# The attention's output projection as a streamed Strassen step, its weight sums made in DRAM, and the FFN's token halves exchanged

## The chip, the cores and the metric

The kernel runs on one core of a Trainium2 chip. The metric is the device time of one execution in microseconds (us), as the median of several. The engines are PE (TensorE: matrix products, and transposes by an identity), DVE (VectorE), ACT (ScalarE) and POOL (GpSimd); SP (SyncE) starts most transfers and does no arithmetic. Each engine works through its own list of instructions in order, and waits at an instruction until what it needs is there.

## The reference

One decoder block in fp32 on `x` of 1024 tokens by 1024 features, with a memory of 256 tokens:

```python
h = h + hybrid_mixer(rmsnorm(h, norm_mix), ...)              # two branches, merged @ w_o
h = h + mem_cross_attention(rmsnorm(h, norm_xattn), rmsnorm(mem, norm_mem), w_xq, w_xkv, w_xo)
h = h + swiglu(rmsnorm(h, norm_ffn), w_ffn_in, w_ffn_out)
return rmsnorm(h, norm_final)

def mem_cross_attention(n, m, w_xq, w_xkv, w_xo):            # 4 heads of 256
    q = (n @ w_xq).reshape(Bsz, S, 4, 256)
    k, v = jnp.split(m @ w_xkv, 2, axis=-1)
    s = jnp.einsum('bshd,bmhd->bhsm', q, k) * 256 ** -0.5
    p = jax.nn.softmax(s, axis=-1)
    o = jnp.einsum('bhsm,bmhd->bshd', p, v).reshape(Bsz, S, 1024)
    return o @ w_xo

def swiglu(n, w_ffn_in, w_ffn_out):
    g, u = jnp.split(n @ w_ffn_in, 2, axis=-1)
    return (jax.nn.silu(g) * u) @ w_ffn_out
```

The change concerns `o @ w_xo`, the residual sum behind it and the way into the FFN.

## The kernel before, in words

**Precision and layout.** Activations lie transposed, features on the 128 partitions and tokens along the row; a "half" is 512 tokens (`HALF`). Each operand of a product is split into a high part, rounded by ACT to PE's fast fp32 type, and a low part that DVE gets by subtraction (`split`, lines 227 to 233); a product is then three passes, high x high, high x low and low x high.

**Strassen.** Most of the large products are a Strassen-Winograd step: 2 x 2 blocks, seven block products (B11, B21, T1, B22, T2, T3, T4) in place of eight. `Wide` and its child `Stored` (lines 1222 to 1366) stream one for a 1024 x 1024 weight matrix: a product has two parts of 24 matmuls (`steps`), each prepared by `prep`, three parts ahead of PE: two DVE sums at most to form the right operand from quadrants (`COMB`), and a split of 128x1024 for either operand. `Stored` reads the sums of weight blocks that the products T1, T2, T3 and B22 need from a DRAM tensor, `sums_d`, that `weight_sums` (line 482) has filled by eight transfers on POOL's queue, twelve in fact since the accumulating ones are cut in two, each behind the one whose result it adds to. Each of the 28 results of 128x512 goes through `evac`: added on DVE onto its output quadrant (`home`), which starts as the block of the residual stream where there is one (`base`); when an output tile is complete, `post` is called. `w_o` goes that way (`wo`, with the mixer's input as base), and the attention's queries too (`xq`).

**The attention** (lines 1601 to 1675) goes over four heads, two token halves each: `score` (PE product, DVE maximum, ACT exponential, DVE division `pe<-pe,sm`), `turn` (PE transposes of the probabilities; then ACT and DVE split them to `phl`), `value` (PE product with `kvhl`; then `into` splits the result, ACT and DVE, into `hl`). The loop is staggered: in step n the scores of one head half, the transposes of the one before and the values of the one before that.

**Its output projection** (lines 1721 to 1725) is a plain product, `dense`: 16 output tiles of 128x512, 24 matmuls each. `Left` brings the weights in column pairs and splits them (`wd`, 128x1024), `residual` adds each result on DVE onto a tile `ga` of `h1_d`, stores it to `h2_d`, has ACT scale a copy for the FFN (`put_xo`, tiles `o`), and adds its square to the sum of squares `ssum` (`Stats.take`). `Stats` sends an add to POOL or DVE, whichever by the planner's running tally is free sooner.

**The FFN** takes its right operand from `Operands` (line 239; tiles B11h, B11l and so on: 28 steps, each a split and for some products a DVE combination); `B.upto(n)` makes steps ahead while the projection is running. Its weights are loaded by `Unit` and split to `whi` and `wlo` (`raw` and `sa` are the weights and their sums). `ffn_side` finishes the norm's statistics after a few of the FFN's steps.

**What sets the order.** The program is written out in Python in the order of its loops; within it `ahead()` raises the rank of an operation (splits, sums and evacuations of the streamed step), and `pinned` fixes one at its place. So the order in which DVE meets preparation, softmax and evacuation is a product of the scheduler. In the trace the DRAM tensors are shortened, `h_d` for `h1_d` and `h2_d`.

## Time and profile before

| what | value |
|---|---|
| time, median of 3 runs | 1927.17 us (1926.22 to 1928.36) |
| the profiled execution's own time | 1924.97 us |
| its span, first to last instruction | 1923.3 us |
| mean granted PE clock | 0.999 |
| PE busy | 1893.0 us, 98% of the span |
| DVE busy | 1361.0 us, 71% |
| ACT busy | 882.0 us, 46% |
| POOL busy | 515.0 us, 27% |
| the `w_xo` projection's matmuls on PE | 1172 to 1270 us, the first 77 among the last value products |

The profile's first part gives busy time, share of the span and number of instructions of each engine; the table by stage gives the same for a stretch of the execution, from:to in us, then its length, each engine's busy time with the count, the granted clock, the DMA engines' busy share and GB/s. A row of the groups has line, engine, operation, output<-input by the program's names, shapes and count; after the bar the summed busy time in us and the mean of one in ns, and after the second bar the engine's idle time just before such an instruction and what ended it. A row of the timeline has start, length, engine and the number of instructions alike in a row. A row of the chain of waits has start, length, and what was waited for.

### The profile page before, as it was taken

The page shows a single profiled execution, that of the slowest core. Times are in us where ns is not written, and L with a number is a line of the kernel's source. Part 1 is how long each engine was busy: PE and PEld are TensorE (multiplying, and loading weights), DVE is VectorE, ACT ScalarE, POOL GpSimd, SP SyncE. Part 2 cuts the span into 40 slices and gives each one's busy share as a digit, 9 for nine tenths or more (in the row PEclk, how much of TensorE's full clock was granted, in tenths as well). Part 3 has the DMA queues.
Part 4 walks back from the last instruction along what each step waited for, and adds up shares of the span by engine and source line. Part 5 has one row for each costly group of instructions (what it writes and reads, how often), then busy time and mean ns, then how long its engine had stood idle before and what let it go on. Part 6 is the DMA issues. An engine that isn't in the chain of part 4 may idle for free.

```text
span 1923.3 us, 26086 instructions
## 1 busy us (share of the span) xinstructions
PE 1893.0 (98%) x9680; PEld 1595.1 (83%) x9680; DVE 1361.0 (71%) x1948; ACT 882.0 (46%) x1521; POOL 515.0 (27%) x410
## 2 busy tenths in 40 slices
PE   7999999999999999999999999999999999999998
PEld 7998787888888888788888888888888888888888
DVE  7866879877776755553479685686878877866566
ACT  7534564564553444652136654553333333344243
POOL 0012324345444221001112000016454535330002
PEclk9999999999999999999999999999999999999999
DMA  9433383455643653898774510425666556397463
GB/s 344 147 95 102 127 306 107 147 177 178 192 154 121 208 181 115 313 328 227 216 191 133 194 58 4 156 98 139 190 174 153 158 168 168 111 300 257 163 220 122
DMA packets 240243, 333.70 MB, mean 174 GB/s; under 512 B 16346, under 2 KB 147652, under 8 KB 240116
## 3 DMA queue, kind: packets, MB, share of 16 engines
q1 hardware_dynamic: 223988, 290.09, 44.8%
q0 software_dynamic: 14400, 35.65, 9.2%
q10 hardware_dynamic: 1728, 6.29, 0.8%
q8 instruction: 76, 1.25, 0.3%
q14 instruction: 51, 0.42, 0.1%
HBM read 242.53 MB, written 120.91 MB: 189 GB/s over the span
## 4 chain that ended last, share of the span: by engine, by line
PE 86%; DVE 7%; issue 2%; DMA 2%; ACT 1%; POOL 1%; SPq 0%; POOLq 0%; DVEq 0%; ACTq 0%
PE acc L51 69%; PE bank L51 15%; DVE cv L73 2%; DVE wlo L73 2%; PE bank L55 2%; DVE o L73 1%; DVE hs L73 1%; DMA hl<-ys_d 0%; DMA zr<-sz_d 0%; DMA down_d<-in_w_ffn_out_dram 0%; POOL ssum L73 0%; ACT cv L783 0%; DMA sz_d<-zr 0%; DVE gy L73 0%; DMA mt<-in_mem_dram 0%
## 5 line engine op out<-in xcount | busy, mean ns | idle before, releaser
L73 DVE TENSOR_TENSOR wlo<-raw,whi 128x512 fp32r<-128x512 f32 x272 | 242.4, 899 | 99.7 <-ACT whi L232 99.7
L232 ACT ACTIVATE whi<-raw 128x512 fp32r<-128x512 f32 x272 | 169.4, 629 | 251.9 <-PE acc L51 210.1
L51 PE MATMUL acc<-hl,wd 128*128 128x512 f32 x1152 | 263.8, 390 | 1.7 <-ACT wd L232 1.3
L51 PEld LDWEIGHTS acc<-hl,wd 128*128 128x128 f32 x1152 | 215.5, 188 | 48.3 <-ACT wd L232 2.5
L73 DVE TENSOR_TENSOR o<-acc,o 128x512 f32<-128x512 f32 x244 | 167.0, 685 | 88.5 <-PE acc L51 85.7
L51 PE MATMUL acc<-fs 128*128 128x512 f32 (+1 forms) x792 | 155.7, 355 | 0.1
L51 PEld LDWEIGHTS acc<-fs 128*128 128x128 f32 x792 | 130.7, 189 | 20.8 <-issue 0.5
L73 DVE TENSOR_TENSOR fs<-fr,fs 128x1024 fp32r<-128x1024 f32 (+1 forms) x78 | 93.1, 1225 | 37.0 <-ACT fs L232 36.6
L232 ACT ACTIVATE fs<-fr 128x1024 fp32r<-128x1024 f32 (+1 forms) x78 | 74.3, 984 | 92.8 <-PE acc L51 27.4
L73 POOL TENSOR_TENSOR sa<-raw 128x512 f32<-128x512 f32 x43 | 68.4, 1592 | 146.2 <-DMA raw<-in_w_in_dram 75.4
L232 ACT ACTIVATE whi<-sa 128x512 fp32r<-128x512 f32 x96 | 59.8, 626 | 96.0 <-PE acc L51 92.7
L73 POOL TENSOR_TENSOR raw<-raw,sa 128x512 f32<-128x512 f32 x35 | 46.0, 1313 | 172.9 <-DVE wlo L73 172.9
L51 PE MATMUL acc<-ws 128*128 128x512 f32 x384 | 88.5, 389 | 0.0
L51 PEld LDWEIGHTS acc<-ws 128*128 128x128 f32 x384 | 72.0, 188 | 15.0
L51 PE MATMUL acc<-T4h,whi 128*128 128x512 f32 x192 | 76.3, 397 | 2.9 <-DVE o L73 2.9
L51 PE MATMUL acc<-B22h,wlo 128*128 128x512 f32 x192 | 75.7, 394 | 1.5 <-DVE wlo L73 1.5
L73 DVE TENSOR_TENSOR wlo<-sa,whi 128x512 fp32r<-128x512 f32 x96 | 70.9, 739 | 8.4 <-ACT whi L232 7.5
L51 PE MATMUL acc<-T1h,whi 128*128 128x512 f32 x192 | 76.2, 397 | 0.0
L51 PE MATMUL acc<-T3h,whi 128*128 128x512 f32 x192 | 76.0, 396 | 0.0
L51 PE MATMUL acc<-T2h,whi 128*128 128x512 f32 x192 | 75.8, 395 | 0.0
L51 PE MATMUL acc<-B22h,whi 128*128 128x512 f32 x192 | 75.7, 394 | 0.0
L73 POOL TENSOR_TENSOR rstd<-rstd,mhalf 128x4 f32<-128x4 f32 (+1 forms) x7 | 8.7, 1252 | 248.1 <-DVE rstd L73 248.1
(420 smaller groups left out, 5007.6 us busy)
## 6 DMA issues: line engine op xcount, KB each, us to landing
raw<-in_w_in_dram SPq DMA_DIRECT2D x26, 1024.0 KB, 5.8
raw<-in_w_ffn_in_dram SPq DMA_DIRECT2D x22, 1024.0 KB, 8.0
act_d<-o SPq DMA_DIRECT2D x77, 256.0 KB, 4.6
fr<-act_d SPq DMA_DIRECT2D x35, 512.0 KB, 7.6
down_d<-in_w_ffn_out_dram POOLq DMA_DIRECT2D x18, 768.0 KB, 7.2
fr<-down_d SPq DMA_DIRECT2D x20, 512.0 KB, 5.3
ga<-h_d SPq DMA_DIRECT2D x32, 256.0 KB, 3.6
csb<-cs_d SPq DMA_DIRECT2D x15, 512.0 KB, 4.3
```

What stands on the lines that cost most here:

```text
L51: return s.e.matmul(o, x, y, **kw)
L55: return s.e.transpose(o, x, i)
L73: return f(*a, **kw)
L232: pin(ACT.activation(hi, src, AF.Copy))
```

## The change

The weight sums for `w_xo` are made in a new DRAM tensor `xos_d` by the same twelve POOL transfers, started from step 3 of the query projection. The output projection becomes a `Stored` step `xo` with `h1_d` as base: `value` no longer splits its result but has ACT copy it into quadrants (`xo.rows`); the first two weight blocks are loaded in steps 3 and 4 of the attention, the first two parts prepared in steps 7 and 8. The output quadrant (1,0) lies in the former `ga` tiles, loaded one by one (`Row`). `post_xo` does what `residual` and `put_xo` did. The FFN's operands exchange the token halves (`swap=1`), so that they follow the order in which the Strassen step finishes its output, and are made two steps at a time from step 8 on. The FFN's first weight loads come one step sooner, its statistics two steps later, and the squares get six buffers (`Stats(rp, "ga", 6)`).

```diff
--- before.py
+++ after.py
@@ -103,6 +103,7 @@
     h1_d = dram("h1_d", D, TOK)
     h2_d = dram("h2_d", D, TOK)
     xqs_d = dram("xqs_d", 2 * D, HALF)
+    xos_d = dram("xos_d", 2 * D, HALF)
     xbc_d = dram("xbc_d", 1536, TOK)
     sz_d = dram("sz_d", D, TOK)
     q_d = dram("q_d", 512, TOK)
@@ -1218,6 +1219,14 @@
     HOME = ("aux", "aux", "m", "m")
     JS = (0, 1)
 
+    class Row:
+
+        def __init__(s, get):
+            s.get = get
+
+        def __getitem__(s, k):
+            return s.get(k[1] if isinstance(k, tuple) else k)
+
     class Wide:
 
 
@@ -1267,6 +1276,9 @@
                     s.plus(name, 2)
 
         def home(s, *ij, fill=True):
+            if ij not in s.keep and s.side[ij] == "ga":
+                s.keep[ij] = Row([quad(s.base, ij[0] * HALF + u * P, 0, ij[1]) for u in range(4)].__getitem__)
+                s.full.add(ij)
             if ij not in s.keep:
                 s.keep[ij] = slot(s.side[ij], (P, 4, HALF), name="wk")
             if fill and s.base is not None and ij not in s.full:
@@ -1364,6 +1376,9 @@
 
         def fetch(s, m, kp):
             s.load(*s.SEQ[:m + 3])
+            if s.base is not None:
+                for ij in {0: ((0, 0), (1, 1)), 2: ((0, 1),), 8: ((1, 0),)}.get(2 * m + kp, ()):
+                    s.home(*ij)
 
     class Left:
 
@@ -1431,7 +1446,7 @@
             yield
 
     EVEN, ODD = ("op",) * 8, ("op",) * 6 + ("aux",) * 2
-    i_ys, i_yg, i_q, i_xo = (paired(x) for x in (EVEN, ODD, EVEN, EVEN))
+    i_ys, i_yg, i_q = (paired(x) for x in (EVEN, ODD, EVEN))
 
     def fetch(src, dst, gain=None):
 
@@ -1522,14 +1537,6 @@
                 x.prep(ops.index(n) + 1, pin)
             yield
 
-    def residual(store, stats, gain, put, scale=1.0):
-        def post(o, j, p, q):
-            DVE.scalar_tensor_tensor(q, p, scale, q, ALU.mult, ALU.add)
-            SP.dma_start(store[o * P:(o + 1) * P, half(j)], q)
-            put(o, j, q, col(gain, o))
-            stats.take(j, q)
-        return post
-
     xq = Stored(t["w_xq"], lambda o, h, p, last: into(i_q, o, h, p, neg=last),
                 {"B11": "m", "T1": "m", "B21": "m", "*": "aux"}, {(0, 0): "m", (1, 1): "m", (0, 1): "aux"})
     xq.sums_d = xqs_d
@@ -1588,14 +1595,25 @@
         split_kv(es, pinned)
         yield
 
-    left_xo = Left((t["w_xo"],))
-
-    def next_left():
-        left_xo.upto(2)
-        yield
-
-    run(xq.steps(), (xq_side(), 1.0), (kv_side(), 1.0), (waiting(next_left(), 12), 1.0))
-    u_xo_stats = Stats(rp)
+    xsums = weight_sums([(t["w_xo"].rearrange("(j k p) c -> j p k c", j=2, p=P), xos_d, 4, 0)])
+    run(xq.steps(), (xq_side(), 1.0), (kv_side(), 1.0), (waiting(xsums, 3), 1.0))
+    drain(xsums)
+    u_xo_stats = Stats(rp, "ga", 6)
+    o_xo = {}
+
+    def row_xo(o):
+        if o // 2 not in o_xo:
+            o_xo[o // 2] = slot(HOME[o // 2], name="o")
+        return o_xo[o // 2][:, o % 2]
+
+    def post_xo(o, h, q, last):
+        SP.dma_start(h2_d[o * P:(o + 1) * P, half(h)], q)
+        ACT.activation(row_xo(o)[:, half(h)], q, AF.Copy, scale=col("norm_ffn", o))
+        u_xo_stats.take(h, q)
+
+    xo = Stored(t["w_xo"], post_xo, {"T2": "aux", "B21": "aux", "*": "m"},
+                {(0, 0): "m", (1, 1): "aux", (0, 1): "aux", (1, 0): "ga"}, h1_d)
+    xo.sums_d = xos_d
 
     class Att:
 
@@ -1652,7 +1670,7 @@
                     for x, y in ((kvh, ph), (kvl, ph), (kvh, pl_)):
                         PE.matmul(p, x[:, 2 + b, i * P:(i + 1) * P], y[:, b], start=m == 0, stop=m == 5)
                         m += 1
-                into(i_xo, 2 * s.h + i, s.j, p)
+                ACT.activation(xo.rows(2 * s.h + i, s.j), p, AF.Copy)
 
     pe = {}
     at = [Att(h, j) for h in range(4) for j in (1, 0)]
@@ -1672,6 +1690,10 @@
             b.turn(1)
         if a:
             a.score(1)
+        if n in (3, 4):
+            xo.load(xo.SEQ[n - 3])
+        if n in (7, 8):
+            xo.prep(n - 6)
 
 
     rbc2 = u_xo_stats.sum
@@ -1715,23 +1737,17 @@
         if u < 2:
             gate.e = up.e = DVE
         gu.append([gate, up])
-    o_xo = [slot(x, name="o") for x in HOME]
-    b_xo = blocks(o_xo)
-
-    def put_xo(o, j, q, g):
-        ACT.activation(b_xo[o][:, half(j)], q, AF.Copy, scale=g)
-
-    B = Operands(b_xo, 4, order=("B11", "T1", "B21", "B22", "T2", "T3", "T4"))
-    for n, _ in enumerate(dense(0, i_xo, residual(h2_d, u_xo_stats, "norm_ffn", put_xo), quad_of(h1_d), js=(1, 0), left=left_xo)):
+    B = Operands(lambda: Row(row_xo), 4, swap=1, order=("B11", "T1", "B21", "B22", "T2", "T3", "T4"))
+    for n, _ in enumerate(xo.steps()):
         if n >= 8:
-            B.upto(n - 7)
-        if n == 12:
+            B.upto(2 * n - 14)
+        if n == 11:
             gu[0][0].load()
-        if n == 14:
+        if n == 13:
             gu[0][1].load()
 
     def ffn_side():
-        for _ in range(2):
+        for _ in range(4):
             yield
         u_xo_stats.close(0)
         yield
```

How it moves instructions, at three places. The first is DVE's list at the end of the attention, on which PE's last value products wait. Before it reads (each tile with its number: `pe` are probabilities and `sm` their sums, `phl` the split probabilities, `hl` the split attention output, `ga` the residual tiles):

```order
L73 TENSOR_TENSOR hl_10384<-bank_10377,hl_10384 128x512
L73 RECIPROCAL sm_10499<-sm_10499 128x2
L73 TENSOR_SCALAR pe_10348<-pe_10348,sm_10499 128x256 x2
L73 TENSOR_TENSOR hl_10394<-bank_10387,hl_10394 128x512
L73 TENSOR_TENSOR phl_10401<-bank_10371,phl_10401 128x512
L73 TENSOR_TENSOR phl_10401<-bank_10372,phl_10401 128x512
L73 TENSOR_TENSOR hl_10384<-bank_10456,hl_10384 128x512
L73 TENSOR_TENSOR hl_10394<-bank_10465,hl_10394 128x512
L73 TENSOR_TENSOR phl_10478<-bank_10450,phl_10478 128x512
L73 TENSOR_TENSOR phl_10478<-bank_10451,phl_10478 128x512
L73 TENSOR_TENSOR hl_10518<-bank_10511,hl_10518 128x512
L73 TENSOR_TENSOR hl_10528<-bank_10521,hl_10528 128x512
```

and now, from the last head half but one (`wr` is a weight block, `ws` a split part, `rq` a quadrant of the attention's output, `wk` an output quadrant, `acc` and `bank` results in PSUM):

```order
L73 TENSOR_TENSOR rq_10138<-rq_10379,rq_10138 128x1024
L73 TENSOR_TENSOR ws_10597<-rq_10138,ws_10597 128x1024
L73 TENSOR_SCALAR pe_10343<-pe_10343,sm_10490 128x256 x2
L73 TENSOR_TENSOR ws_10639<-wr_10559,ws_10639 128x1024
L73 SCALAR_TENSOR_TENSOR wk_10561<-acc_10558,wk_10561 128x512
L73 TENSOR_TENSOR ws_10640<-rq_10379,ws_10640 128x1024
L73 TENSOR_TENSOR ws_10669<-wr_10559,ws_10669 128x1024
L73 TENSOR_TENSOR rq_10062<-rq_10379,rq_10062 128x1024
L73 TENSOR_TENSOR rq_10138<-rq_10379,rq_10138 128x1024
L73 TENSOR_TENSOR ws_10670<-rq_10379,ws_10670 128x1024
L73 TENSOR_TENSOR phl_10528<-bank_10502,phl_10528 128x512
L73 TENSOR_TENSOR phl_10528<-bank_10503,phl_10528 128x512
```

The splits `hl` of the attention's output are gone from between the `phl` splits; in their place stand weight and quadrant splits, quadrant sums and evacuations of the projection, ahead of the last scaling `pe` and of the last `phl`.

The second is PE's list at the same place. Before (`hl,wd` are matmuls of the dense projection):

```order
L51 MATMUL acc<-hl,wd 128x512 x29
L55 MATMUL bank<-ident,pe 128x128 x4
L51 MATMUL acc<-hl,wd 128x512 x3
L55 MATMUL bank<-ident,pe 128x128 x3
L51 MATMUL bank<-phl,kvhl 128x512 x12
L55 MATMUL bank<-ident,pe 128x128
L51 MATMUL acc<-hl,wd 128x512 x19
L55 MATMUL bank<-ident,pe 128x128 x4
L51 MATMUL acc<-hl,wd 128x512 x2
```

and now (`ws` are matmuls of the streamed step):

```order
L51 MATMUL acc<-ws 128x512 x21
L55 MATMUL bank<-ident,pe 128x128 x2
L51 MATMUL acc<-ws 128x512 x15
L51 MATMUL bank<-phl,kvhl 128x512 x5
L51 MATMUL acc<-ws 128x512 x9
L51 MATMUL bank<-phl,kvhl 128x512 x7
L51 MATMUL acc<-ws 128x512 x3
L55 MATMUL bank<-ident,pe 128x128 x4
L51 MATMUL bank<-phl,kvhl 128x512 x10
L51 MATMUL bank<-ws 128x512 x12
```

The first product of the projection (B11), 48 matmuls, stands ahead of the last head half's transposes (`ident,pe`, four); before, 53 of the dense projection stood around the transposes of the last two head halves.

The third is POOL's list behind the norm statistics of the queries (`rstd`), now:

```order
L73 TENSOR_TENSOR rstd<-rstd,mhalf 128x4 x2
L73 DMA xos_d<-in_w_xo_dram 128x4x512 x2
L73 DMA xos_d<-in_w_xo_dram 128x2x512 x4
L73 DMA xos_d<-xos_d 128x4x512
L73 DMA xos_d<-in_w_xo_dram 128x4x512
L73 DMA xos_d<-in_w_xo_dram 128x2x512 x2
L73 DMA xos_d<-xos_d 128x2x512 x2
L73 TENSOR_TENSOR ssum<-ssum,sq 128x512 x10
L73 TENSOR_TENSOR rstd<-rstd,mhalf 128x4 x2
```

Before, four `rstd` operations stood there in a row, without a transfer or an add between them: the twelve transfers (rows x2, x4, one, one, x2, x2) are new, and ten of the adds of the squares (`ssum`), all 14 of which DVE did, are now POOL's.

## The prediction

> **What bounds the kernel now.** I read the totals and the chain of waits first, then the table by stage, then the groups of instructions of the two stages that matter, then single rows.
>
> ```profile
> PE 1893.0 (98%) x9680; PEld 1595.1 (83%) x9680; DVE 1361.0 (71%) x1948; ACT 882.0 (46%) x1521; POOL 515.0 (27%) x410
> PE 86%; DVE 7%; issue 2%; DMA 2%; ACT 1%; POOL 1%; SPq 0%; POOLq 0%; DVEq 0%; ACTq 0%
> core 0: us, PE busy (x) PEld busy (x) DVE busy (x) ACT busy (x) POOL busy (x), PEclk, DMA share, GB/s
> 984.00:1060.00 76.00, 76.00 (x337) 62.91 (x336) 62.47 (x66) 42.89 (x58) 17.39 (x11) 1.00 0.56 157
> 1141.00:1206.00 65.00, 63.01 (x343) 52.77 (x341) 38.38 (x91) 33.75 (x82) 0.00 (x0) 1.00 0.08 26
> 1170.00:1296.00 126.00, 125.48 (x575) 103.35 (x574) 85.33 (x137) 62.07 (x112) 8.28 (x5) 1.00 0.29 96
> 1266.00:1276.00 10.00, 10.00 (x46) 8.29 (x45) 10.00 (x18) 10.00 (x20) 0.00 (x0) 1.00 0.16 58
> 1276.00:1286.00 10.00, 10.00 (x54) 8.52 (x53) 10.00 (x19) 4.23 (x9) 1.61 (x1) 1.00 0.63 207
> 1286.00:1296.00 10.00, 10.00 (x53) 8.40 (x52) 9.89 (x13) 5.92 (x10) 6.67 (x5) 1.00 0.01 2
> ```
>
> PE is busy for 98% of the span, so a matmul less is time less, unless another engine takes its place. The stages are: 984 to 1060 the streamed Strassen step for `w_o`, which is what the change makes of the `w_xo` step; 1141 to 1206 the end of the attention; 1170 to 1296 the last of it, the whole `w_xo` projection and the FFN's start. In that last stretch PE idles for 0.5 us of 126, and DVE has 40.7 us free; but in its last 30 us DVE is already full, and PE is not yet waiting.
>
> **The term that is removed.** The dense projection has 384 matmuls of 512 columns, the Strassen form 7 x 48 = 336.
>
> ```profile
> 1027.30 24.48 PE acc L51 x108
> 1179.96 2.77 PE bank L51 x12
> 1187.18 0.44 PE bank L55 x4
> 1143.04 3.95 PE acc L51 x33
> ```
>
> In the chain of waits (start, us, what, count) 108 matmuls of the `w_o` step take 24.48 us, 0.2267 each: 48 fewer are **10.9 us**. The other rows give 0.231 for a value matmul, 0.11 for a transpose and 0.12 for a score matmul of 256 columns. If nothing else changed, 1924.97 us of the profiled execution would be 1914.1; the median lies 2.2 us above that execution, and I carry this difference along.
>
> **What DVE gets.** The groups below are those of the `w_o` step, then those of 1170 to 1296; last come rows of the timeline, whose starts show the pace.
>
> ```profile
> L73 DVE TENSOR_TENSOR ws<-wr,ws 128x1024 fp32r<-128x1024 f32 x12 | 16.2, 1352 | 8.2 <-ACT ws L232 8.2
> L73 DVE TENSOR_TENSOR ws<-rq,ws 128x1024 fp32r<-128x1024 f32 x11 | 13.9, 1262 | 0.0
> L73 DVE TENSOR_TENSOR rq<-rq 128x1024 f32<-128x1024 f32 x8 | 12.1, 1533 | 0.1
> L232 ACT ACTIVATE ws<-wr 128x1024 fp32r<-128x1024 f32 x12 | 12.6, 1049 | 9.5 <-DMA wr<-in_w_o_dram 9.3 <-DVE ws L73 0.2
> L73 DVE SCALAR_TENSOR_TENSOR ga<-acc,ga 128x512 f32<-128x512 f32 x16 | 11.0, 689 | 13.3 <-PE acc L51 11.0 <-DMA ga<-h_d 2.3
> L73 DVE TENSOR_TENSOR ssum<-ssum,sq 128x512 f32<-128x512 f32 x14 | 9.6, 689 | 3.5 <-ACT sq L524 3.5
> L73 DVE TENSOR_TENSOR wd<-raw,wd 128x1024 fp32r<-128x1024 f32 x6 | 7.2, 1222 | 0.5 <-ACT wd L232 0.5
> L73 DVE TENSOR_TENSOR hl<-bank,hl 128x512 fp32r<-128x512 f32 x8 | 5.5, 689 | 17.5 <-ACT hl L232 17.5
> 1038.44 0.68 DVE L73 SCALAR_TENSOR_TENSOR wk<-acc,wk 128x512 f32<-128x512 f32 x1
> 1039.04 1.22 DVE L73 TENSOR_TENSOR ws<-wr,ws 128x1024 fp32r<-128x1024 f32 x1
> 1040.17 1.22 DVE L73 TENSOR_TENSOR ws<-rq,ws 128x1024 fp32r<-128x1024 f32 x1
> ```
>
> One after the other, a 128x512 operation costs DVE 0.60 us (1039.04 - 1038.44) and a 128x1024 one 1.13 (1040.17 - 1039.04). The new step adds 28 splits and 8 quadrant sums of 128x1024 and 28 evacuations of 128x512: 36 x 1.13 + 28 x 0.60 = 57.5 us. Out of the stretch go 16 residual evacuations (`ga`), 8 attention splits (`hl`; eight more lie earlier), 6 weight splits (`wd`) and ten of the 14 square sums (`ssum`, to POOL): 34 x 0.60 + 6 x 1.13 = 27.2. DVE's work there becomes 85.3 + 57.5 - 27.2 = 115.6 us, and without its 48 matmuls the stretch is 115.1 us long.
>
> The ten adds on POOL are not free for DVE.
>
> ```profile
> 1041.91 6.21 DVE L73 TENSOR_TENSOR rq<-rq 128x1024 f32<-128x1024 f32 x3
> 1048.04 2.31 DVE L73 TENSOR_TENSOR ws<-wr,ws 128x1024 fp32r<-128x1024 f32 x1
> 1039.99 9.27 POOL L73 TENSOR_TENSOR ssum<-ssum,sq 128x512 f32<-128x512 f32 x4 [21.83 <-ACT sq L524]
> 1054.70 1.36 POOL L73 TENSOR_TENSOR ssum<-ssum,sq 128x512 f32<-128x512 f32 x1 [0.87 <-ACT sq L524]
> ```
>
> While POOL ran four of them, four DVE operations took 8.5 us in place of 4.5: about 1.0 us lost for each add. Over the whole `w_o` step, 33 long and 33 short DVE operations would take 57.1 us at their pace and took 62.47: 5.4 us for six adds, 0.9 each. I take 0.9 x 10 = 9 us; the bounds are nothing and 10 x 1.36 = 13.6, the add's own shortest duration. So DVE has 124.6 us to do in 115.1, about **9.5 us too much**.
>
> The Trainium skill (SBUF — State Buffer, section "SBUF: two separate sides") speaks against this move: it calls the port pair of the two engines an exclusive lock, so that a DVE operation with two SBUF inputs waits for the whole of a POOL one that reads SBUF. By that rule I would take the upper bound, 13.6, and the time would be 4.6 us longer than by the 0.9 of the row.
>
> ACT does not become the bound: 28 splits of 1.05 us come, 16 of 0.6 and 8 long ones go, about 12 us on top of 62.07 in 126.
>
> **Where PE would wait.** Its instruction order shows the place. The first three products' preparation stands in DVE's queue ahead of the last head's softmax scaling and of its last `phl` split, on which PE's last value matmuls wait; PE's queue is in order, so the projection behind them waits too. From the end of the first half of the fifth head's-half value block (about 1170 by the rows above and the earlier stages) PE has 66 matmuls (15.0 us), 12 transposes (1.3) and 9 score matmuls (1.1) in hand: 17.4 us. DVE must first do 18 long operations, six of 128x512 and the small softmax ones (1.4): 20.4 + 3.6 + 1.4 = 25.4, beginning some 1.6 us later (a value copy and one 1.05 split on ACT), and then one `phl` split, 0.6: 27.6. **PE idles 10 us**, bounds 3 (if half of these eighteen run in DVE's earlier gaps; it is idle for 26.6 of 65 us in the attention's end) and 12. The count of DVE's surplus gave 9.5: I take the two as one wait seen twice, since DVE, never idle from there, has its surplus paid at this place.
>
> Sum: -10.9 - 0.5 (the idle time of today) + 10 = -1.4; 1923.6 in the profiled terms, **1925.8** for the median.
>
> **The weight sums in DRAM.** Twelve POOL transfers, each waiting for the one before, as the present ones for `w_xq`:
>
> ```profile
> L73 POOL DMA_DIRECT2D xqs_d<-in_w_xq_dram x9: 782/1144/1207, 858.4 to 935.0; - x9
> DMA to landing us min/median/max: 5.3/7.8/10.0
> 1084.80 2.03 POOL L73 TENSOR_TENSOR rstd<-rstd,mhalf 128x4 f32<-128x4 f32 x2 [28.74 <-DVE rstd L73]
> 1100.00:1120.00 20.00, 20.00 (x90) 16.57 (x89) 17.55 (x24) 11.24 (x16) 0.00 (x0) 1.00 0.38 124
> 1140.00:1160.00 20.00, 19.24 (x127) 17.03 (x126) 15.95 (x44) 14.32 (x43) 0.00 (x0) 1.00 0.08 27
> raw<-in_w_ffn_in_dram SPq DMA_DIRECT2D x22, 1024.0 KB, 8.0
> ```
>
> They stand behind POOL's `rstd` of 1084.8, so they begin at 1087, where PE has no use for POOL and the DMA share falls from 0.38 to 0.08: they cost nothing while hidden. At 5.3 to 7.8 us each they end between 1151 and 1181; the third product's load waits for the last one and lands up to 8.0 later, 1159 to 1189. DVE comes to it at 1170 + 1.6 + 17.5 = 1189. So the cover just holds by the median, with room by the lower row. SP's queue is in order: the load of `h1_d`, the base of the evacuations, and later loads stand behind that wait.
>
> The Trainium skill (DMA: Bandwidth & Descriptors, section "Anatomy of one DMA — SWDGE (gpsimd) path") fits such a transfer as 2.0 us plus bytes over 436 GB/s; by it the chain would take an estimated 43 us and end at 1130. The quickest one here took 5.3 us where that gives 3.2, so the row decides.
>
> **The rest at nothing:** exchanging the FFN's token halves reorders as many products; preparing the FFN's operands at two a step moves DVE work from the FFN's start into the projection, within the same 126 us; the gate and up loads come a step earlier, under a DMA share of 0.16. If the latter were uncovered, one 8.0 us landing would show.
>
> **The rivals.**
>
> A, *the whole gain*. The `w_o` step is the same code, with DVE 82% busy and PE without a gap (76.00 of 76.00): DVE's earlier idle time takes the preparation, and the work too much slips behind 1296. Then -10.9 - 0.5: 1915.8. Against it: DVE's order, and that `w_o` has no attention in front. Between A and the forecast lies a tail wait of 3 to 7 us: 1918.8 to 1922.8.
>
> B, *the FFN's start waits too; slower*. DVE is full there today for 30 us (10.00, 10.00, 9.89). If the wait at the attention's end doesn't pay the surplus (the DVE operations there wait for PE in turn), DVE comes to the FFN's first splits with the 9 us that POOL took still undone, and PE stops for them between the last projection matmuls and the second FFN product: 1925.8 + 9 = 1935. It decides as soon as PE's idle time in the stretch passes 11.4 us. Against it: 12 of 28 operand splits done by the projection's end, where it was 8.
>
> C, *the sums come late; slower*. At 10.0 us each, as their slowest, they end at 1207 and the load at 1215, 26 us after DVE wants it; 10 of these lie under the tail wait already counted: 1942. Against it: the DMA share. That the change doesn't do what it says I leave out, as the order has the 336 matmuls.
>
> **How the numbers follow.** What a measurement can't tell from no change is 0.2%, 3.9 us: 1923.3 to 1931.0. Forecast 0.40, within it. A 0.20, and the cases between A and the forecast 0.16: faster 0.36. B 0.16 and C 0.08: slower 0.24. The forecast's own range is 1922.8 (tail wait 7) to 1931 (tail wait 12 and a few us at the FFN's start). Range: 1916 to 1935, from A to B; C and the outer halves of A and B are left out, some 0.2.
>
> **What would show it.** Right: PE idle for about 10 us in one or two gaps around 1185 to 1200, ended by DVE `phl` or `pe`; DVE busy for over 95% from 1170 to 1290; the projection's last matmul near 1265 and the FFN's first ones without a gap; 12 `xos_d` issues from 1087 with the last before 1181; DVE operations beside POOL's `ssum` near 2 us. Wrong: `phl` in time and PE at 10.00 in every slice there (A); PE idle ended by DVE `wlo`, `B22l` or the like after 1260 (B); an idle time of ACT or DVE ended by DMA `wr<-xos_d` (C).

## The result, and the profile after

The changed kernel takes 1950.12 us (median of 4 runs, 1949.28 to 1952.81) against 1927.09 before: a ratio of 1.0121 with a 95% interval of 1.0104 to 1.0139. It is 23 us slower; 1925.8 was forecast, in a range of 1916 to 1935. The profiled execution of it took 1952.81 us, with a span of 1951.1.

Three marks in the trace cut the span into stretches that can be compared: PE's first score product of the attention, its first matmul of the FFN, the first one of product T4 in the FFN's first unit, and the first one of the down projection. All stretches of this document are differences of these starts.

| us | attention and projection | FFN's first unit, up to T4 | rest of the FFN's units |
|---|---|---|---|
| before | 143.1 | 36.5 | 384.8 |
| after | 140.7 | 46.7 | 401.7 |
| difference | -2.4 | +10.2 | +16.9 |

The rest lies ahead of the attention, which begins at 1130.1 rather than 1126.9; later executions, of the kernel before with small edits too, began it between 1127.7 and 1130.3, so that this is not the change. So the stretch in which 48 matmuls (10.9 us) were saved is 2.4 us shorter, and the FFN behind it 27 us longer.

The totals of the page, and the table by stage (from:to, length, busy time of PE, PEld, DVE, ACT and POOL with the count of each, granted clock, DMA share, GB/s; PEld are PE's weight loads), after:

```profile
PE 1894.7 (97%) x9632; PEld 1592.5 (82%) x9632; DVE 1383.3 (71%) x1962; ACT 901.3 (46%) x1541; POOL 538.4 (28%) x432
1130.00:1206.00 76.00, 68.33 (x410) 59.67 (x409) 61.01 (x124) 49.85 (x111) 5.42 (x5) 0.93 0.45 128
1206.00:1256.00 50.00, 50.00 (x222) 41.42 (x221) 37.72 (x44) 28.39 (x40) 5.17 (x4) 1.00 0.43 147
1256.00:1306.00 50.00, 43.35 (x181) 33.90 (x180) 48.86 (x75) 29.09 (x51) 15.05 (x8) 0.93 0.32 105
```

and the same of before:

```profile
1130.00:1206.00 76.00, 74.01 (x432) 63.57 (x430) 47.47 (x118) 40.98 (x106) 0.00 (x0) 1.00 0.07 23
1256.00:1306.00 50.00, 50.00 (x237) 41.77 (x236) 41.31 (x64) 26.14 (x46) 13.99 (x9) 1.00 0.26 86
```

PE has 48 matmuls less and still 1.7 us more busy time: part of its matmuls ran at a lower granted clock, 0.93 over the two stretches in which it also idles, 7.7 us to 1206 and 6.7 us from 1256 on. DVE has 13.5 us more to do in the first, and is full in the second.

Where PE waits, from the timeline after (start, length, what, count; in brackets the idle time before and who ended it):

```profile
1192.53 0.70 PE L55 MATMUL bank<-ident,pe 128*128 128x128 f32 x4 [1.83 <-DVE pe L73]
1200.80 2.93 PE L51 MATMUL bank<-phl,kvhl 128*128 128x512 f32 x6 [4.92 <-DVE phl L73]
1259.85 11.16 PE L51 MATMUL acc<-ws 128*128 128x512 f32 x48 [1.09 <-DVE wk L73]
1276.79 0.47 PE L51 MATMUL acc<-T1h,whi 128*128 128x512 f32 x1 [2.60 <-DVE ga L73]
1288.04 2.48 PE L51 MATMUL bank<-ones,ssum 128*128 128x1 f32 x16 [1.02 <-DVE ssum L73]
1299.06 0.50 PE L51 MATMUL acc<-B22h,whi 128*128 128x512 f32 x1 [1.21 <-ACT whi L233]
1372.07 0.50 PE L51 MATMUL acc<-B21h,wlo 128*128 128x512 f32 x1 [2.27 <-DVE wlo L73]
1396.07 0.80 PE L51 MATMUL acc<-T1h,whi 128*128 128x512 f32 x1 [7.84 <-ACT whi L233]
```

There are three groups. At 1192 and 1200 PE waits for the last head's scaling and `phl` split, which stand behind the projection's preparation in DVE's list. From 1259 to 1299 it waits for evacuations, splits and sums of a DVE that is full. And at 1372 and 1396, well into the FFN, it waits for weights that ACT and DVE make. PE's waits from 1300 to 1730 (us in total, times, longest), first after, where ACT's are the largest, then before, where there is one:

```profile
PE acc L51 <- ACT whi L233: 8.7, 2, 7.8
PE acc L51 <- DVE o L73: 0.9, 1, 0.9
```

The wait of 7.84 us is read from POOL and ACT:

```profile
1384.19 1.27 POOL L73 DMA_DIRECT2D down_d<-in_w_ffn_out_dram  x1
1392.31 1.24 POOL L73 DMA_DIRECT2D down_d<-down_d  x1 [6.84 <-issue]
1393.10 1.74 POOL L73 TENSOR_TENSOR o<-o,ssum 128x512 f32<-128x512 f32 x1
1394.87 0.63 ACT L1704 ACTIVATE o<-o 128x512 f32<-128x512 f32 x1 [13.75 <-POOL o L73]
1395.41 0.61 ACT L233 ACTIVATE whi<-sa 128x512 fp32r<-128x512 f32 x1
```

`down_d` are sums of the down projection's weight blocks, 32 transfers on POOL's queue that are made beside the FFN, in the kernel before as well. POOL stands for 6.84 us ahead of such a transfer; behind it in POOL's list is a product of the gate with the norm (`o<-o,ssum`), behind that in ACT's list its SiLU, and behind that the split `whi` that PE needs.

From 1193.70, from 1289.27 and from 1391.67 on the granted clock is at half, for 10.2, 6.8 and 10.2 us. The table by stage of the first two of these stretches, and then two rows of PE's timeline from the third:

```profile
1193.70:1203.94 10.24, 5.22 (x11) 3.65 (x12) 9.90 (x11) 2.65 (x4) 0.00 (x0) 0.50 0.38 125
1289.27:1296.10 6.83, 6.83 (x21) 5.57 (x21) 6.83 (x13) 1.71 (x3) 0.15 (x1) 0.50 0.46 154
```

```profile
1400.21 0.63 PE L51 MATMUL acc<-T1h,wlo 128*128 128x512 f32 x1
1400.63 0.63 PE L51 MATMUL acc<-T1h,whi 128*128 128x512 f32 x1
```

Matmuls then follow each other at 0.42 us (1400.63 - 1400.21) rather than 0.227: some 11 of them after 1193, 13 after 1290 and 12 after 1396, 0.2 each, together 7 us of the 23.

### The profile page after: what moved, and what is told of

It is laid out like the page before. It is cut to its first block, busy times and chain, and to the rows that moved or that the text cites. A ratio compares the mean times of both kernels' runs of the same rounds, so it can differ in the third digit from the quotient of the medians.

```text
span 1951.1 us, 26054 instructions
## 1 busy us (share of the span) xinstructions
PE 1894.7 (97%) x9632; PEld 1592.5 (82%) x9632; DVE 1383.3 (71%) x1962; ACT 901.3 (46%) x1541; POOL 538.4 (28%) x432
## 5 line engine op out<-in xcount | busy, mean ns | idle before, releaser
L51 PE MATMUL acc<-hl,wd 128*128 128x512 f32 x768 | 174.7, 389 | 1.5 <-ACT wd L233 1.1
L51 PEld LDWEIGHTS acc<-hl,wd 128*128 128x128 f32 x768 | 143.9, 188 | 32.3 <-ACT wd L233 1.7
L51 PE MATMUL acc<-ws 128*128 128x512 f32 x576 | 133.9, 390 | 1.4 <-DVE wk L73 1.1
L51 PEld LDWEIGHTS acc<-ws 128*128 128x128 f32 x576 | 107.7, 188 | 24.5 <-issue 1.5
L51 PE MATMUL bank<-ws 128*128 128x512 f32 x432 | 99.8, 390 | 0.0
L51 PEld LDWEIGHTS bank<-ws 128*128 128x128 f32 x432 | 81.4, 188 | 17.0
L73 POOL TENSOR_TENSOR ssum<-ssum,sq 128x512 f32<-128x512 f32 (+1 forms) x24 | 38.2, 1591 | 196.9 <-ACT sq L525 184.4
L73 DVE TENSOR_TENSOR o<-o,ssum 128x512 f32<-128x512 f32 x67 | 65.9, 984 | 35.4 <-ACT o L1704 34.1
L51 PE MATMUL acc<-B21h,wlo 128*128 128x512 f32 x192 | 76.3, 399 | 2.3 <-DVE wlo L73 2.3
L51 PE MATMUL acc<-T1h,wlo 128*128 128x512 f32 x192 | 76.4, 398 | 1.9 <-DVE wlo L73 1.9
```

Source lines behind the costliest of these rows:

```text
L51: return s.e.matmul(o, x, y, **kw)
L73: return f(*a, **kw)
```

## The experiments

All times stand against runs of the kernel before on the same chip (medians from 1926.5 to 1927.5). The stretches, from the profiled executions:

| kernel | time | attention and projection | FFN's first unit | rest of the units |
|---|---|---|---|---|
| sums alone | 1927.1 | 143.1 | 36.5 | 384.2 |
| later `down_d` | 1965.0 | 141.6 | 46.7 | 412.1 |
| squares on DVE | 1956.6 | 142.5 | 49.2 | 402.7 |
| three parts from step 6 | 1948.8 | 139.0 | 46.4 | 398.8 |
| spread `down_d` | 1935.9 | 145.0 | 44.6 | 383.9 |
| spread, second unit on POOL | 1939.3 | 144.4 | 48.7 | 383.7 |
| the last, and four parts from step 5 | 1930.8 | 135.1 | 48.1 | 383.6 |
| before, spread `down_d` | 1925.9 | 143.1 | 36.5 | 383.7 |
| v1: spread, four parts | 1928.4 | 133.7 | 46.4 | 384.4 |
| v2: v1, operand sums on POOL | 1934.5 | 135.4 | 51.2 | 383.8 |
| v3: v1 without the adds of squares | 1920.5 | 134.3 | 40.9 | 384.0 |
| v4: v1, operands at the old pace | 1927.5 | 135.3 | 45.7 | 384.0 |

**The weight sums alone**, in the kernel before:

```diff
+    xsums = weight_sums([(t["w_xo"].rearrange("(j k p) c -> j p k c", j=2, p=P), xos_d, 4, 0)])
-    run(xq.steps(), (xq_side(), 1.0), (kv_side(), 1.0), (waiting(next_left(), 12), 1.0))
+    run(xq.steps(), (xq_side(), 1.0), (kv_side(), 1.0), (waiting(xsums, 3), 1.0), (waiting(next_left(), 12), 1.0))
+    drain(xsums)
```

> The kernel before with one part of the change alone: the twelve transfers that sum the blocks of w_xo into the new DRAM tensor, beside the query projection; nobody reads the sums, the dense projection stays. If the sums are covered (my theory), the time is that of before, 1927 us within 2 us, and the twelve transfers are over by about 1165 us. If they themselves disturb the queries or the attention, through POOL's queue or the DMA engines, it is slower by more than 4 us. The changed kernel reaches the attention 3.2 us later than the one before: if that comes from the sums or from the new tensor's place in memory, it shows here too (1930 us).

1927.09 us, ratio 0.9999 (0.9990 to 1.0008). The last transfer was issued at 1159.45:

```profile
1089.00 0.84 POOL L73 DMA_DIRECT2D xos_d<-in_w_xo_dram  x1
1159.45 1.14 POOL L73 DMA_DIRECT2D xos_d<-xos_d  x1 [4.44 <-issue]
```

The sums cost nothing. Their 12 transfers took 76 us, issue to issue 5.5 to 7.7 us each, within the 64 to 94 us that twelve times the 5.3 to 7.8 us of the `w_xq` rows had given, and not the 43 of the fit.

**The sums of `w_ffn_out` later**, as a test of the third group of waits:

```diff
-        run(group([gate], B, () if last else gu[u + 1][:1]), (last_sums, 0.4))
+        run(group([gate], B, () if last else gu[u + 1][:1]), *([(last_sums, 0.55)] if u > 2 else []))
         for n, _ in enumerate(group([up], B, () if last else gu[u + 1][1:])):
-            if n == 2:
+            if n == 2 and u > 2:
```

> The changed kernel, with the sums of the blocks of w_ffn_out (down_d, on POOL's queue, each behind the landing of the one before) begun at the FFN's fourth unit rather than its second. Theory: the FFN's loss between 1317 and 1719 us (16.9 us against before) is POOL standing at such a transfer with the products of the gate behind it, whose lateness holds ACT and then PE; with the transfers later, the gap of 7.8 us before 1396 and the one of 2.3 before 1372 go, and the time falls by 11 to 16 us, to 1934 to 1939. Rival: the FFN waits for weights or operands because of the exchanged halves, and the time stays at 1950 within 2 us. Second rival: the same gap moves to where the transfers then lie, and the time stays as well, with the gap after 1450.

1965.01 us, 15 us slower than the changed kernel: the theory in this form fell, and the second rival, the waits moving with the transfers, held in part, as the time did not stay but grew. No wait of PE's is left from 1317 to 1400, and seven come behind. To end in time the transfers had been put closer (4.8 for a unit rather than 3.8), and POOL's timeline shows:

```profile
1403.83 0.80 POOL L73 DMA_DIRECT2D down_d<-in_w_ffn_out_dram  x1
1412.34 1.33 POOL L73 DMA_DIRECT2D down_d<-in_w_ffn_out_dram  x1 [5.55 <-issue]
1420.12 1.27 POOL L73 DMA_DIRECT2D down_d<-in_w_ffn_out_dram  x1 [3.27 <-issue]
1427.83 0.78 POOL L73 DMA_DIRECT2D down_d<-down_d  x1 [6.44 <-issue]
```

The same kernel's view of waits, from 1300 to 1730 (us in total, times, longest):

```profile
PE acc L51 <- ACT whi L233: 19.2, 7, 3.3
```

From the first of these four transfers to the last are 24 us (1403.83 to 1427.83), in which POOL does three operations of its own and stands for 15.3 us ahead of transfers (5.55 + 3.27 + 6.44). PE waits for ACT seven times, 19.2 us, where the changed kernel had two such waits of 8.7 us together. Beginning the transfers later does not help when more of them then come in the same time.

**The sums spread**: eight of the 32 transfers during the projection, the others 2.4 for a unit.

```diff
     for n, _ in enumerate(xo.steps()):
+        if n < 8:
+            next(last_sums)
...
-        run(group([gate], B, () if last else gu[u + 1][:1]), (last_sums, 0.4))
+        run(group([gate], B, () if last else gu[u + 1][:1]), (last_sums, 0.2))
```

> The changed kernel with the sums of the blocks of w_ffn_out drawn apart: the first eight of the 32 transfers during the projection, one a step, where POOL is idle, the rest in the FFN at 2.4 for each unit of it rather than 3.8. In the changed kernel, and more so with the sums crowded into later units (1965 us), POOL issues three or four in a row, and each waits some 8 us for the landing of the one before while a product of the gate stands behind it. Theory: apart, they hold nobody; the stretch from the first unit's last product to the down projection, 401.7 us against 384.8 before, falls to 384 to 388, and the time to 1933 to 1938. Rival: the crowding is a mark of POOL being late for another reason, and the stretch stays above 398, the time at 1947 to 1952.

1935.85 us, ratio 1.0047 (1.0032 to 1.0062), 14.3 us below the changed kernel. The stretch fell from 401.7 to 383.9; in the same view of waits there is left

```profile
PE acc L51 <- DVE wlo L73: 1.0, 1, 1.0
```

The theory held, within its numbers: as they lay, the transfers were worth the 17 us. The edit makes them both fewer beside the FFN (24 rather than 32) and further apart, and does not tell which of the two counts. It isn't free: attention and projection became 4.3 us longer, with larger waits at 1200 (5.6) and before the projection's last product (3.2), the latter followed by matmuls at half clock.

**The control: the same spreading in the kernel before.**

```diff
     for n, _ in enumerate(dense(0, i_xo, residual(h2_d, u_xo_stats, "norm_ffn", put_xo), quad_of(h1_d), js=(1, 0), left=left_xo)):
+        if n < 8:
+            next(last_sums)
...
-        run(group([gate], B, () if last else gu[u + 1][:1]), (last_sums, 0.4))
+        run(group([gate], B, () if last else gu[u + 1][:1]), (last_sums, 0.2))
```

> The control for the spread sums: the same spreading in the kernel before, with its dense projection. If the crowding of the transfers hurts only behind the late start of the FFN that the change brings, there is nothing to gain here: 1927 us within 2 us. If they hold PE up in the kernel before as well, this is faster by more than 2 us.

1925.94 us, ratio 0.9994 (0.9985 to 1.0003): nothing to gain. In the kernel before POOL stands at such transfers too, but PE's waits there came to 0.9 us. The change made PE wait for a POOL that it had not waited for.

**The preparation earlier**: three parts from step 6 on.

```diff
-        if n in (7, 8):
-            xo.prep(n - 6)
+        if n in (6, 7, 8):
+            xo.prep(n - 5)
```

> The changed kernel with the first three parts of the projection prepared in steps 6, 7 and 8 of the attention's loop rather than the first two in steps 7 and 8, so that DVE, which is only 60 to 70% busy from 1146 to 1176, takes some of that work earlier. Theory: the gaps of PE at the attention's end (7.7 us of idle time and about 2.5 us of matmuls at half the granted clock) fall by half or more, 4 to 8 us, and the time to 1942 to 1946. Rival: DVE's surplus only moves, to the projection's last product and the FFN's start, and the time stays at 1950 within 2 us.

1948.75 us, 1.4 less with overlapping runs (1945.84 to 1951.87 against 1949.28 to 1952.81), so the rival's figure: attention and projection gained 1.7, the wait for `phl` fell from 4.9 to 3.5 and the one before the projection's last product grew from 1.1 to 2.3. Half a step is not enough to bring the softmax ahead in DVE's list. With four parts, in steps 5 to 8, most of the wait goes (below).

**The second unit's weight sums on POOL**, with the spread sums:

```diff
-        if u < 2:
+        if u < 1:
             gate.e = up.e = DVE
```

> As the spread sums, and the weight sums of the FFN's second unit are made on POOL, not on DVE. DVE, full from 1256 to 1306 us, loses eight operations of 128x512 there, about 5 us at 0.60. Theory of DVE's surplus: the stretch from the FFN's first to its first unit's last product, 46.7 us (36.5 before), gets 4 to 6 us shorter, and the time is as much below that of the spread sums alone. Rival: POOL, at 1.3 to 1.7 us an operation and with the norm's rstd behind the sums, becomes what PE waits for, and the stretch is no shorter.

1939.25 us, 3.4 more than with the spread sums alone: the rival held. DVE loses nine operations from 1256 to 1306 and only 2.2 us of busy time, and PE now waits 3.7 us for weights that POOL was to sum. The table by stage, with the spread sums alone and then in this run, and then POOL's timeline:

```profile
1256.00:1306.00 50.00, 42.02 (x172) 32.23 (x172) 48.97 (x76) 30.26 (x55) 15.00 (x8) 0.93 0.32 105
1256.00:1306.00 50.00, 41.21 (x157) 31.82 (x156) 46.80 (x67) 29.30 (x52) 18.84 (x13) 0.87 0.33 105
```

```profile
1290.11 2.29 POOL L73 TENSOR_TENSOR sa<-raw 128x512 f32<-128x512 f32 x1 [9.05 <-DVE B22l L73]
```

**Four parts from step 5**, on top of it:

```diff
-        if n in (7, 8):
-            xo.prep(n - 6)
+        if n in (5, 6, 7, 8):
+            xo.prep(n - 4)
```

> As the run before, and the projection's first four parts prepared in steps 5 to 8 of the attention's loop; in DVE's list the last softmax scaling then stands ahead of most of the projection's preparation. Theory: PE's gaps at the attention's end go (7.7 us idle and 2.5 us at half the granted clock), the attention and the projection together take 131 to 134 us (143.2 before, 140.8 with the change), and the time falls by 6 to 9 us against the run before, to 1921 to 1927. Rival, the surplus only moves: the gap before the projection's last product and the FFN's start grow by as much, and the time gains less than 3 us.

1930.81 us, ratio 1.0017 (1.0007 to 1.0026): 8.4 below the run before, in attention and projection 9.3 (144.4 to 135.1). The gain is of the size that the theory had, 6 to 9; the stretch stayed 1 us above the forecast 131 to 134, and the total is above the forecast 1921 to 1927, which counted on a gain from the run before. Of the waits at the attention's end 2.1 us are left (0.23 and 1.88). The FFN's first unit stayed at 48.1.

**v1: spread sums and four parts**, the second unit's sums back on DVE.

> The changed kernel with two repairs: the sums of w_ffn_out's blocks spread, and the projection's first four parts prepared in steps 5 to 8 of the attention's loop (the run with both and the second unit's sums on POOL gave 1930.8 us, and those sums on POOL cost 3.4). Theory: 1926 to 1929 us, no difference from before: the two gaps are closed, the FFN's start still gives back what the 48 matmuls save. Rival: with the attention's end in order, DVE comes to the FFN's start without arrears, and the stretch there falls from 46 to under 40 us: 1920 or less.

1928.39 us, ratio 1.0009 (1.0000 to 1.0017): as the theory had it, the loss is gone and there is no gain. Attention and projection take 133.7 us, 9.5 less than before, nearly all of the 10.9. The FFN's first unit gives it back. PE's timeline, and the table by stage:

```profile
1252.01 11.16 PE L51 MATMUL acc<-ws 128*128 128x512 f32 x48 [2.48 <-DVE wk L73]
1269.02 0.47 PE L51 MATMUL acc<-T1h,whi 128*128 128x512 f32 x1 [2.67 <-DVE ga L73]
1289.41 0.50 PE L51 MATMUL acc<-B22h,whi 128*128 128x512 f32 x1 [2.54 <-ACT whi L233]
```

```profile
1256.00:1306.00 50.00, 43.28 (x193) 34.20 (x192) 44.30 (x70) 29.87 (x51) 16.80 (x10) 0.97 0.30 95
```

**All adds of squares on DVE**, in the changed kernel, to price the ones on POOL:

```diff
-        u_xo_stats.take(h, q)
+        u_xo_stats.take(h, q, e=DVE)
```

> The changed kernel with all 14 square sums of the projection on DVE, none on POOL. By the 0.9 us that a POOL add took from DVE in the w_o step, DVE gains 9 and has 6 us more to do: the gaps of PE between 1258 and 1300 shrink by about 3 us, the time is 1947. By the rule of an exclusive lock, 13.6 and 6, it is 1942. If POOL costs DVE nothing, DVE has 6 us more to do there and the time is 1954 to 1957.

1956.56 us, 6.4 more: the case in which POOL's adds cost DVE nothing was the one that gave the number, though the trace of the changed kernel contradicts its reason, since an operation of DVE with two inputs in SBUF is slow beside such an add, 1.47 us rather than 0.68:

```profile
1261.07 1.30 POOL L73 TENSOR_TENSOR ssum<-ssum,sq 128x512 f32<-128x512 f32 x1 [8.99 <-ACT sq L525]
1261.44 1.47 DVE L73 TENSOR_TENSOR T1l<-o,T1h 128x512 fp32r<-128x512 f32 x1
```

What made the 6.4 us is open: DVE's busy time from 1256 to 1306 falls, from 48.86 to 47.36 us, and 0.9 us of the loss lies at the attention's end, ahead of the first add (the wait for `phl` is 5.79 rather than 4.92).

**v2: the operand sums of T2, T3 and T4 on POOL**

```diff
-                        comb[0](DVE, q(of), q(comb[1]), q(comb[2]))
+                        comb[0](POOL if s.swap and name in s.order[4:] else DVE, q(of), q(comb[1]), q(comb[2]))
```

> As v1, and the twelve sums of operand blocks for the FFN's products T2, T3 and T4 on POOL, not DVE. DVE loses 12 x 0.60 = 7.2 us between 1255 and 1300; POOL is busy for 15 of 50 us there. Theory of DVE's surplus: PE's gaps at the FFN's start shrink by 3 to 7 us, 1921 to 1925. Rival: each sum on POOL takes 1.3 to 1.7 us, twelve of them 16 to 20, and DVE is held up by them about 0.8 each; the products then wait for POOL, and the time is that of v1 or above.

1934.48 us, 6.1 above v1: the rival held. Table by stage and timeline of v2:

```profile
1256.00:1306.00 50.00, 40.72 (x172) 32.79 (x171) 47.14 (x56) 25.99 (x46) 30.15 (x19) 0.90 0.29 95
```

```profile
1269.06 1.70 POOL L73 TENSOR_TENSOR ssum<-ssum,sq 128x512 f32<-128x512 f32 x1
1270.72 1.71 POOL L73 TENSOR_TENSOR o<-o 128x512 f32<-128x512 f32 x1
1269.56 1.74 DVE L73 TENSOR_TENSOR B22l<-o,B22h 128x512 fp32r<-128x512 f32 x1
1271.23 0.68 DVE L73 SCALAR_TENSOR_TENSOR ga<-acc,ga 128x512 f32<-128x512 f32 x1
```

DVE has 56 operations in place of v1's 70, and is busy for 47.1 us in place of 44.3. An operation with two inputs in SBUF takes 1.74 us beside POOL, one with an input in PSUM (`ga<-acc,ga`) 0.68 in the midst of it.

**v3: without the adds of squares**

```diff
-        u_xo_stats.take(h, q)
+        if u_xo_stats.n[h] == 0:
+            u_xo_stats.take(h, q)
```

> As v1, with the 14 adds of squares left out on both engines (the norm's statistics then hold one tile of eight in each half, so the output is another). It measures what they cost: by 0.60 for each of the four on DVE and 0.8 to 0.9 for each of the ten on POOL, DVE gains 10 to 11 us between 1236 and 1290, and the gaps there go from about 8 us to nearly nothing: 8 us below v1 or more. If POOL's adds cost DVE little, as the run with all of them on DVE suggests, it is 2 to 4 us.

1920.49 us, 7.9 below v1 and 0.34% below before (0.9966, 0.9952 to 0.9979). The edit leaves out the 14 squares on ACT as well, 0.62 us each. One of the 14 with its add is worth 0.6 us of time; the FFN's first unit is 5.5 us shorter (40.9), and the waits before the projection's last product and behind it are gone. Taking work out of that stretch is thus time. That it is DVE's and POOL's work rather than ACT's is argued and not tested by itself: in v1 DVE is busy for 44.3 and ACT for 29.9 of the 50 us.

```profile
1256.00:1306.00 50.00, 45.30 (x202) 35.79 (x201) 41.17 (x67) 25.15 (x43) 9.33 (x7) 1.00 0.25 86
```

**v4: the FFN's operands at the old pace**

```diff
-            B.upto(2 * n - 14)
+            B.upto(n - 7)
```

> As v1, with the FFN's operands prepared at one step of 28 for each step of the projection, as in the kernel before, not two (6 done by the projection's end rather than 12). Theory: DVE's work in the stretch is the same, so the gaps only change place: the ones before the projection's last product and behind it (2.5 and 2.7 us in v1) shrink, those in the FFN's first products grow by as much, and the time is v1's within 2 us, 1926.5 to 1930.5. Rival: the early operands get in the way of the evacuations PE waits for, and without them 3 to 5 us are gained, 1923 to 1925. Second rival: doing them early is what saves the FFN's start, and the time is 4 us or more above v1's.

1927.50 us, ratio 1.0005 (0.9996 to 1.0014), 0.9 from v1 with overlapping runs: the total is as the theory said. Its detail is not: of the waits of 2.48 and 2.67 us before the projection's last product and behind it, the first did not shrink and the second shrank by 0.4. The early operands neither save the FFN's start nor cause these two waits.

No run of these is faster than the kernel before beyond the measurement but v3, which leaves work out. The exchange of the token halves was not tried by itself.

## Why the prediction was wrong

**The saving: right.** 48 matmuls at 0.2267; v1 gets 9.5 of the 10.9 us in its stretch.

**The attention's end: right in place, mechanism and size.** Forecast were 10 us of idle time behind DVE's preparation, ended by `pe` and `phl`. Measured were 0.36, 1.83, 0.58 and 4.92, 7.7 in all, and some 2.2 us of matmuls at half the clock; the stretch became 2.4 us shorter where -1.4 was forecast. The wait was 2.3 us smaller than forecast, and the clock, which the sum lacked, put about as much in its place. Preparing earlier (x_all) left 2.1 us of the wait, in the way that the bound of 3 us had named.

**The sums in DRAM: right**, and covered; the last landing came before 1170.

**POOL's adds: right in kind, too large.** 0.9 us each, 9 in all, was taken from the `w_o` step. In the changed kernel DVE's operations beside the ten adds took 6.8 us longer than the usual 0.68 for 128x512 and 1.21 for 128x1024. An add beside operations with an input in PSUM cost next to nothing, as the one of 1262.93 beside two of `wk<-acc,wk` (0.68 and 0.67 us). In time, all 14 squares and their adds left out (v3) are worth 0.6 each, and moving the ten to DVE (x_ssum_dve) cost 0.6 each more. The Trainium skill's exclusive lock (SBUF — State Buffer, "SBUF: two separate sides") is borne out by v2 in what it slows, two SBUF inputs but not one, and about in its size: 1.06 us lost (1.74 - 0.68) of POOL's 1.3 to 1.7. As a price of the ten adds the upper bound of 13.6 was twice what they cost.

**The step that failed first: "I take the two as one wait seen twice".** DVE's surplus of 9.5 us and the wait of 10 at the attention's end were the same size, and were taken for one. They are two. DVE's balance by stage in the changed kernel, and what ended most of its idle time from 1206 to 1256 (us in total, times, longest):

```profile
1176.00:1204.00 28.00, 20.33 (x80) 15.26 (x79) 27.61 (x33) 16.23 (x23) 0.00 (x0) 0.82 0.32 112
1250.00:1300.00 50.00, 43.35 (x179) 33.92 (x177) 49.65 (x74) 33.02 (x58) 13.87 (x10) 0.93 0.35 117
DVE wk L73 <- PE bank L51: 9.1, 3, 5.4
```

While PE stood at the attention's end, DVE did work of the projection's first products, without a break (27.61 of 28 us), and then idled from 1206 to 1256 for 12.3 of 50 us, most of it waiting for results to evacuate. The work of the last third, evacuations, splits of 28 operands, their sums and two units of weights, stands behind that, and much of it needs the projection's results. There DVE is full again (49.65 of 50 us), and the surplus is paid once more, at the FFN's start: +10.2 us, close to the rival B's 9, which had a chance of 0.16. The average over 126 us hid two full stretches with an idle one between them. v1 shows that they are two: with the first wait repaired, the second stretch stays at 46.4. That DVE's work makes the second is borne out by v3, where it falls to 40.9 with work left out; x_ssum_dve, where DVE's busy time fell and the time rose, says that the busy time alone does not give the size.

**The step that failed worst: "the rest at nothing".** The FFN's other units, unchanged by the diff, lost 16.9 us. The prediction looked at POOL's list up to `rstd` and not at what stands behind it: the transfers of `down_d` had been holding POOL in the kernel before, without harm. With the FFN's first unit 10 us longer and its statistics two steps further back, products of the gate that PE soon needs come behind them. That POOL's transfers are the cause is shown (later and closer +15 us, spread -14.3, in the kernel before nothing). Which part of the change made them harmful, the longer first unit, the two steps or the exchanged halves, stays open. The start of the FFN alone is not it: with three parts from step 6 its first matmul comes at 1267.14, before the 1270.05 of the kernel before, and the other units still take 398.8 us. No rival had it, as all ended at the FFN's start.

In the sum: 3.2 us ahead of the attention, -2.4, +10.2 and +16.9 on 1924.97 make 1952.9; the profiled execution took 1952.81.

## What to carry to other kernels

An engine's free time counts only where its inputs are ready: make the balance by stage, and when a surplus and a wait come out alike, ask whether the work behind the wait could be done in it at all. A change that delays a stage also delays what that stage feeds, so follow each engine's list past the edit, above all queues that stand at transfers: what is harmless while nobody waits (the same transfers of `down_d` before) can become a wait when the work around it moves. And price a gap of PE with the matmuls behind it at half the clock.

## What the runs showed of the hardware

**The granted clock falls when PE idles for part of a few microseconds**, and stays at 0.50 for 3.4, 6.8 or 10.2 us, even if PE is busy by then. The Trainium skill (TensorE: Matmul & The Clock Gate, "Part 1: The HAM clock gate") has the clock at half after an idle window of about 3.4 us. The measurement differs in that the window need not be idle throughout: the 3.41 us ahead of the fall at 1193.70 hold 2.30 us of idle PE (3.41 - 1.11). And a wait of 2.33 us in x_all was followed by 48 matmuls in 12.76 us, one of 2.48 us in v1 by 48 in 11.16. The granted clock shows why: in each run the falls between 1110 and 1720 lie whole multiples of 3.41 us apart, as those of the changed kernel at 1193.70, 1289.27 and 1391.67 (28 and 30 times 3.413), so that time is cut into stretches of 3.41 us. In x_all the wait lies in one such stretch (2.33 us idle), and the clock falls at its end. In v1, with the stretches counted back from its fall at 1270.93, it is cut in two (0.92 and 1.56 us idle), and the clock stays. The row of the changed kernel, then x_all, then v1:

```profile
1190.29:1193.70 3.41, 1.11 (x6) 0.40 (x4) 3.41 (x5) 3.17 (x6) 0.00 (x0) 1.00 0.65 240
1250.98 12.76 PE L51 MATMUL acc<-ws 128*128 128x512 f32 x48 [2.33 <-DVE wk L73]
1248.36:1251.77 3.41, 1.08 (x6) 0.69 (x5) 3.41 (x6) 0.90 (x2) 0.00 (x0) 1.00 0.02 8
1251.77:1255.18 3.41, 3.41 (x10) 2.64 (x9) 3.41 (x6) 3.14 (x6) 2.42 (x2) 0.50 0.39 146
1247.04:1250.45 3.41, 2.49 (x11) 1.72 (x10) 3.41 (x5) 2.27 (x5) 0.00 (x0) 1.00 0.00 0
1250.45:1253.87 3.42, 1.86 (x8) 1.59 (x9) 3.42 (x7) 1.94 (x4) 0.65 (x1) 1.00 0.20 77
```

Idle time isn't all of it: the fall at 1289.27 followed a stretch with 1.02 us of it, at whose end 16 matmuls of one column (`ones,ssum`, from 1288.04) were running.

**A transfer of POOL mostly starts only after the one before has landed, but not always.** The first two copies into `xos_d` have different targets and were issued 6.7 us apart, while landing takes 5.2 to 8.3 us; in x_bspread two first copies into `down_d` were issued within 1.6 us, and in the changed kernel two at 1465.35 and 1466.13. What held the ones and not the others the profile doesn't show. The rows of the changed kernel, and then of x_bspread:

```profile
1090.02 0.84 POOL L73 DMA_DIRECT2D xos_d<-in_w_xo_dram  x1
1096.76 0.78 POOL L73 DMA_DIRECT2D xos_d<-in_w_xo_dram  x1 [5.90 <-issue]
1089.47 1.60 POOL L73 DMA_DIRECT2D down_d<-in_w_ffn_out_dram  x2
```

Where such a transfer is held, all that stands behind it in POOL's list waits too, 4.5 to 7.4 us for each of the `xos_d` transfers of 0.5 to 1 MB behind the first.
